# Feed-forward: the second matrix by two-by-two blocks, seven block products for eight, for four of its eleven pairs of row tiles

## The chip, the cores and the metric

The kernel runs on one NeuronCore of a Trainium2 chip. The metric is the device time of one execution in microseconds (us); the kernel before takes 1118.28 us (median of three runs, 1118.25 to 1118.4). The engines are called as the profile calls them: PE (TensorE), PEld (its weight loads), DVE (VectorE), ACT (ScalarE), POOL (GpSimd), SP (SyncE, which issues the DMAs).

## What is computed

Two layers on a sequence of 256 tokens, 1024 wide. Each layer is feed-forward, mixer, feed-forward, each followed by a layer norm; the mixer of the first layer is a hybrid of two recurrent branches, that of the second a sparse attention. So there are six stages: feed-forward, hybrid mixer, feed-forward, feed-forward, sparse attention, feed-forward. The change is in the feed-forward, which the reference writes as

```python
def swiglu(x, w_in, w_out):
    gate, up = jnp.split(x @ w_in, 2, axis=-1)
    return (jax.nn.silu(gate) * up) @ w_out

h = layer_norm(DEEPNORM_ALPHA * h + 0.5 * swiglu(h, ffn_w_in[layer, 0], ffn_w_out[layer, 0]), ...)
```

`w_in` is 1024 x 5632 (gate and up, 2816 columns each), `w_out` is 2816 x 1024. All is fp32.

## The kernel before

**Precision.** A matrix product of fp32 values is made of three products of a rounded type (fp32r): each operand is split into `hi` (rounded) and `lo` (the rest), and `mm3` issues hi·hi, hi·lo and lo·hi into one PSUM bank. `split` makes the two halves: `hi` is a copy that the planner may give to ACT or to DVE (an `alts` entry), `lo` is a subtraction on DVE. Weights come by DMA into a tile `raw` (4 buffers of 1 MB, each 128 x 2048) and are split into `whi` and `wlo`, tiles of 128 x 1024 out of a pool `m4` of 36 buffers, which nearly all other large tiles share.

**The feed-forward (`ffn`).** The 2816 inner columns are 22 row tiles `f` of 128 (NF = 22), taken in pairs `s` = 0 to 10. For each `f`, `proj_two` makes the gate and the up projection, one after the other, each into one of two PSUM banks `ps`: 8 matmuls of 512 columns and 8 of 256. `add_two` reads a bank (an ACT copy of one half, a DVE addition of the other), ACT applies silu, DVE multiplies, and the result is split into a pair tile `g` (hi and lo, 256 tokens each). Then `out_mm` multiplies `g` with two row tiles of `w_out`: for each token half b (128 tokens) and each output half c (512 columns) one `mm3` into one of the four banks `acc[b][c]`, 3 matmuls of 128 x 128 by 512 columns; 12 matmuls for a row tile, 24 for a pair. The products of a pair are issued in turn with the projections of the next. For the last `LAG` = 5 row tiles (8 in the last stage) the products of b = 1 are kept back to the end of the stage, so that the layer norm of b = 0 (`then(0, acc)`) can run beneath them.

**The layer norm** of a half reads `acc` into a tile `h` with `scalar_tensor_tensor` (0.5 · acc + `ah`, the scaled input), takes statistics, scales, and `transpose_half` transposes `h` through a bank `mp` (two of these) and splits it into the next stage's `x`. PSUM is full: 2 `ps`, 2 `mp`, 4 `acc`.

**The order.** Nothing is issued as it is written. `Plan` records each operation, and `order` sorts them by a list schedule: for each engine the operation that can start first, and among those the one recorded earliest. It has its own prices, knows the dependencies and the buffers, and gives `m4` buffers by stream under `QUOTAS`: stream W (weights) may hold 12 buffers while an earlier tile of another stream still waits for one, else 24; stream G (the tiles `g`) 4. `emit` then issues the sorted operations from one line, so that in the profile of before every operation stands at L538 (L540 in the changed file) and tiles, not lines, tell them apart. Tile names: `raw`, `whi`, `wlo` weights; `x` stage input; `ps`, `mp`, `acc` PSUM banks; `sg`, `g` feed-forward products; `h`, `lnst`, `lnmv`, `lnve`, `lng`, `lnb` layer norm.

Of the kernel before, what the change touches and what calls it, by code (L numbers as in the profile page):

```python
# [18 lines left out]
P = 128  # L19
T = 256  # L20
D = 1024
# [10 lines left out]
    "ps": (2, "PSUM"), "mp": (2, "PSUM"), "acc": (4, "PSUM"),  # L32
}

QUOTAS = {"M": None, "D": None, "S": (8, 8), "Z": (4, 4), "L": (4, 4), "G": (4, 4), "P": (5, 5), "Q": (5, 5), "W": (12, 24)}

KEPT = ("L", "G")

SHARE = {"tensor": 1.0}

# [6 lines left out]
}  # L47

ENDS = 3

STRANDS = ("mp",)
W_HYB, W_NSA = (60.0, 140.0, 25.0, 40.0, 15.0), (70.0, 60.0, 40.0, 20.0)
# [509 lines left out]
class K:  # L562
# [3 lines left out]
    def __init__(self, plan, ins, caps):  # L566
        self.nc = self.plan = plan
        self.i = ins
        self.caps = caps
        self.strand = ""  # L570
        self.consts()


# [20 lines left out]
        return v  # L594

    def m4(self, n, name, stream="M", dtype=F32):
        quota = QUOTAS[stream]
# [47 lines left out]
    def unit(self, srcs, parts):  # L645

        raw = self.plan.tile("raw", [P, 2048], F32, "raw", stream="W")
        for dst, src in srcs:
            self.nc.sync.dma_start(dst(raw), src)
        out = []  # L650
        for f in parts:
            v = f(raw)
            n = int(v.ids.size)
            shape = v.shape
            hi = self.m4(n, "whi", "W", F32R)
            lo = self.m4(n, "wlo", "W", F32R)
            if len(shape) == 3:
                hi, lo = (t.rearrange("p (a b) -> p a b", a=shape[1]) for t in (hi, lo))
            self.split(hi, lo, v)
            out.append((hi, lo))  # L660
        return out

# [38 lines left out]
    def first_weights(self, w, c0, arrivals):  # L701

        out = []
        for k0 in range(0, KD, 2):
            if k0 % 4 == 0:
                raw = self.plan.tile("raw", [P, 2048], F32, "raw", stream="W")
            v = H3(raw[:, k0 % 4 * 512:(k0 % 4 + 2) * 512], 2)
            hi, lo = (H3(self.m4(1024, n, "W", F32R), 2) for n in ("whi", "wlo"))
            step = 1 if arrivals and k0 < 4 else 2
            for e in range(0, 2, step):  # L710
                self.nc.sync.dma_start(v[:, e:e + step], w[:, k0 + e:k0 + e + step, c0:c0 + 512])
                self.split(hi[:, e:e + step], lo[:, e:e + step], v[:, e:e + step])
# [219 lines left out]
    def ffn(self, l, j, x, then, last=False):  # L932
# [8 lines left out]
        def gtiles(f):  # L941
            if f // 2 not in pairs:
                pairs[f // 2] = self.m4(1024, "g", "G", F32R).rearrange("p (a t) -> p a t", a=4)
            v = pairs[f // 2]
            return v[:, f % 2 * 2, :], v[:, f % 2 * 2 + 1, :]

        def out_mm(b, f, g, wo, cols=range(2)):
            for c in cols:
# [2 lines left out]
                self.mm3(acc[b][c], (g[0][:, bs], g[1][:, bs]), (wo[0][:, cs], wo[1][:, cs]), f == 0,  # L951
                         f == NF - 1 - (ENDS if last and b == 1 and c == 1 else 0))
        gts = {}
        if self.first:
            self.first_steps(x, w_in, gtiles, gts)
        else:
# [30 lines left out]
        for s in range(NT, DFF // 256):  # L987
            wg = self.unit_cols(w_in, s * 256, 256)
            wu = self.unit_cols(w_in, DFF + s * 256, 256)
            if s == NT:  # L990
                for n in range(NT):
                    wo = self.unit_rows(w_out, 2 * n, 2, 0, D)
                    todo += [(2 * n + e, gts[2 * n + e], wo[e]) for e in range(2)]
            if s == NT + 4:
                self.mark = len(self.plan.ops) - 1
            for e in range(2):
                if e == 1:
                    wo = self.unit_rows(w_out, 2 * s, 2, 0, D)
                f = 2 * s + e
                sg, up = self.pair("sg")  # L1000
                self.add_two(sg, self.proj_two(x, wg[e]))
                nc.scalar.activation(sg, sg, AF.Silu)
                self.add_two(up, self.proj_two(x, wu[e]))
                nc.vector.tensor_tensor(sg, sg, up, OP.mult)
                g = gtiles(f)
                self.split(g[0], g[1], sg)
                if e == 0:
                    hold = (f, g)
                    flush(1)
                else:  # L1010
                    todo.append((*hold, wo[0]))
                    flush(1)
                    todo.append((f, g, wo[1]))
        flush(0)
        then(0, acc)

        ends = late[-ENDS:] if last else []
        for c in range(2):
# [1065 lines left out]
```

## Time and profile before

| | |
|---|---|
| device time, median of 3 runs | 1118.28 us (1118.25 to 1118.4) |
| span of the profiled execution, first to last instruction | 1116.8 us, 1.5 us below the median; the page gives no other time for it |
| PE busy | 1103.7 us (99%), 6545 matmuls |
| DVE busy | 886.6 us (79%) |
| ACT busy | 516.6 us (46%) |
| DMA | 196.80 MB by the SP queue, 53.4% of 16 engines |
| the four feed-forward stages in the trace | 0 to 193 us, 430 to 615, 615 to 800, 925 to the end |

The profile page is read from its first two parts (busy shares) to the chain that ended last: followed back from the last instruction, it tells which engine's work, and of which tiles, the time goes through. Matmuls are pipelined, so that the duration of one (about 0.39 us) is longer than the distance from one to the next; for sums the distance counts, and it is read from stretches of the chain with a count. The same holds, less strongly, on DVE and ACT.

### The profile page before, as it was taken

To read this page: it belongs to the slowest core of one execution; us is meant where nothing else is said; L and a number is where in the kernel's file an instruction comes from. 1 tells how busy PE (TensorE), PEld (TensorE's weight loads), DVE (VectorE), ACT (ScalarE), POOL (GpSimd) and SP (SyncE) were. 2 spreads that over 40 slices of the span, in tenths; PEclk is the share of its full clock that TensorE was granted. 3 is DMA by queue.
4 is the path that set the end of the run, shared out by engine and by line. 5 is a ranking of instruction groups with operands and counts; after the bars stand their busy time and mean duration, and the time that the engine had idled before them with its cause. 6 is when DMAs were issued, how large, how long until landed. Compare 5 with 4: busy or idle time off the path is not lost.

```text
span 1116.8 us, 16492 instructions
## 1 busy us (share of the span) xinstructions
PE 1103.7 (99%) x6545; PEld 944.8 (85%) x6545; DVE 886.6 (79%) x1494; ACT 516.6 (46%) x932; POOL 56.2 (5%) x103
## 2 busy tenths in 40 slices
PE   9999999999999999999999999999999999999997
PEld 7888888899999788888888888888887778888886
DVE  7977768799979999777767977876879979677765
ACT  5635332278736545533433643332456776433320
POOL 1000000012001410000000000000000100000000
PEclk9999999999999999999999999999999999999999
DMA  9876562642923276755664665655426237656511
GB/s 341 302 253 197 184 216 80 188 133 55 271 96 103 88 237 215 264 188 185 193 185 155 230 210 184 211 181 163 141 91 224 76 114 266 224 188 201 176 39 38
DMA packets 147846, 197.84 MB, mean 177 GB/s; under 512 B 9373, under 2 KB 122682, under 8 KB 147770
## 3 DMA queue, kind: packets, MB, share of 16 engines
q1 hardware_dynamic: 147770, 196.80, 53.4%
q8 instruction: 51, 0.84, 0.3%
q14 instruction: 25, 0.20, 0.1%
HBM read 194.04 MB, written 1.05 MB: 175 GB/s over the span
## 4 chain that ended last, share of the span: by engine, by line
PE 87%; DVE 8%; ACT 2%; issue 2%; DMA 1%; POOL 1%; DVEq 0%; ACTq 0%; POOLq 0%
PE ps L538 52%; PE acc L538 31%; PE mp L538 4%; DVE wlo L538 2%; DVE arena L538 1%; DVE cv L538 1%; DMA raw<-in_nsa_w_in_dram 1%; ACT whi L538 1%; DVE o L538 0%; POOL arena L538 0%; DVE whi L538 0%; DVE AT L538 0%; DVE y L538 0%; DVE x L538 0%; DVE h L538 0%
## 5 line engine op out<-in xcount | busy, mean ns | idle before, releaser
L538 DVE TENSOR_TENSOR wlo<-raw,whi 128x1024 fp32r<-128x1024 f32 (+2 forms) x351 | 416.1, 1207 | 11.6 <-ACT whi L538 8.5
L538 PE MATMUL ps<-x,whi 128*128 128x512 f32 (+2 forms) x1584 | 368.8, 363 | 1.4 <-ACT cv L538 1.0
L538 PEld LDWEIGHTS ps<-x,whi 128*128 128x128 f32 (+1 forms) x1584 | 278.8, 188 | 46.1 <-ACT cv L538 3.0
L538 ACT ACTIVATE whi<-raw 128x1024 fp32r<-128x1024 f32 (+2 forms) x258 | 258.6, 1045 | 25.8 <-DMA raw<-in_ffn_w_in_dram 15.6
L538 PE MATMUL acc<-whi,g 128*128 128x512 f32 x698 | 228.5, 391 | 0.0
L538 PE MATMUL ps<-x,wlo 128*128 128x256 f32 x1368 | 222.6, 283 | 0.0
L538 ACT ACTIVATE sg<-ps 128x256 f32<-128x256 f32 x156 | 60.0, 385 | 343.9 <-PE ps L538 343.9
L538 PEld LDWEIGHTS ps<-x,wlo 128*128 128x128 f32 x1368 | 197.7, 190 | 11.3
L538 DVE TENSOR_TENSOR sg<-ps,sg 128x256 f32<-128x256 f32 (+1 forms) x158 | 67.4, 427 | 155.5 <-ACT sg L538 155.1
L538 PEld LDWEIGHTS acc<-whi,g 128*128 128x128 f32 x698 | 131.4, 188 | 25.7
L538 PE MATMUL acc<-wlo,g 128*128 128x512 f32 x349 | 136.9, 392 | 0.0
L538 PE MATMUL ps<-whi,x 128*128 128x512 f32 (+1 forms) x480 | 129.1, 385 | 0.0
L538 PEld LDWEIGHTS ps<-whi,x 128*128 128x128 f32 x480 | 85.9, 188 | 15.3 <-issue 0.8
L538 PEld LDWEIGHTS acc<-wlo,g 128*128 128x128 f32 x349 | 65.8, 189 | 10.8
L538 PE MATMUL acc<-whi,x 128*128 128x512 f32 x224 | 73.5, 404 | 0.4 <-ACT x L538 0.3
L538 PE MATMUL ps<-wlo,x 128*128 128x512 f32 (+1 forms) x240 | 67.4, 381 | 0.0
L538 DVE CAST whi<-raw 128x1024 fp32r<-128x1024 f32 (+2 forms) x93 | 63.4, 681 | 3.7 <-DMA raw<-in_nsa_w_in_dram 3.7
L538 PEld LDWEIGHTS ps<-wlo,x 128*128 128x128 f32 x240 | 43.5, 188 | 7.1
L538 PEld LDWEIGHTS acc<-whi,x 128*128 128x128 f32 x224 | 41.3, 188 | 9.5 <-DVE x L538 1.1
L538 POOL TENSOR_TENSOR lnve<-lnve,mhalf 128x1 f32<-128x1 f32 x12 | 11.5, 956 | 734.5 <-DVE lnve L538 734.5
L538 ACT ACTIVATE sg<-sg 128x256 f32<-128x256 f32 x72 | 30.2, 419 | 33.0 <-DVE sg L538 32.8
L538 PE MATMUL acc<-wlo,x 128*128 128x512 f32 x112 | 43.0, 398 | 0.0
(252 smaller groups left out, 1013.5 us busy)
## 6 DMA issues: line engine op xcount, KB each, us to landing
raw<-in_ffn_w_in_dram SPq DMA_DIRECT2D x72, 1024.0 KB, 5.2
raw<-in_ffn_w_out_dram SPq DMA_DIRECT2D x44, 1024.0 KB, 5.0
raw<-in_hyb_w_in_dram SPq DMA_DIRECT2D x20, 1024.0 KB, 5.3
raw<-in_ffn_w_in_dram SPq DMA_DIRECT2D x30, 512.0 KB, 5.0
raw<-in_hyb_w_out_dram SPq DMA_DIRECT2D x8, 1024.0 KB, 5.0
raw<-in_nsa_w_in_dram SPq DMA_DIRECT2D x5, 1024.0 KB, 5.5
raw<-in_nsa_cmp_w_dram SPq DMA_DIRECT2D x4, 1024.0 KB, 5.2
raw<-in_nsa_w_out_dram SPq DMA_DIRECT2D x4, 1024.0 KB, 6.0
```

The costliest lines, as they stand in the source:

```text
L538: r = getattr(getattr(nc, eng), fn)(*[res(a) for a in args], **{k: res(a) for k, a in kw.items()})
```

## The change

For the pairs s = 4 to 7 (`SEVEN = (4, 8)`) of every feed-forward the two row tiles and the two token halves are treated as a two-by-two block matrix, the two row tiles of `w_out` and the two output halves as another, and their product is made by the Winograd form of Strassen's method: seven block products in place of eight, of sums and differences of blocks.

- `token_forms` makes the sums of token blocks on DVE: four operations on 128 x 128 blocks of a tile `F`, then one hi copy (ACT) and one lo subtraction (DVE) of 7 blocks, 896 columns, into `fhi` and `flo`.
- `weight_forms` makes the sums of weight blocks from one `raw`: `t13` (1024 columns), two additions of 512 into `t24`, and hi and lo halves of 1024, 512, 1024 and 1024 columns. Before, a pair had hi and lo halves of 1024 and 1024.
- The products of these pairs leave the place among the projections and stand at the end of the stage in one run of 84 matmuls, in seven banks: `acc[0][0]`, `acc[0][1]`, `acc[1][0]` and the two `mp` and two `ps`. Pairs 0 to 3 stay where they were; pairs 8 to 10 (`tail`, six row tiles) follow the run, first b = 0 then b = 1, so `LAG` falls away.
- Four products were collected in banks of their own. ACT copies one, and DVE adds them up (`u`: two operations for b = 0, two for b = 1) and adds the four results to `ah` (`put`), before the layer norm reads it.
- In the feed-forward all hi halves of weights and of `g` go to ACT (`hard_split`), while before the planner chose between ACT and DVE.
- Quotas: stream W gets a limit that is written per pair (`most`), G goes from 4 to 20 buffers, and a stream F comes in.

```diff
-QUOTAS = {"M": None, "D": None, "S": (8, 8), ..., "G": (4, 4), ..., "W": (12, 24)}
-KEPT = ("L", "G")
+QUOTAS = {"M": None, "D": None, "F": None, "S": (8, 8), ..., "G": (20, 20), ..., "W": (12, 24)}
+KEPT = ("L", "G", "F")
+SEVEN = (4, 8)
...
+    def hard_split(self, hi, lo, src):
+        self.nc.scalar.activation(hi, src, AF.Copy)
+        self.nc.vector.tensor_tensor(lo, src, hi.bitcast(F32), OP.subtract)
+
+    def weight_forms(self, w, k0):
+        nc, V = self.nc, self.nc.vector
+        raw = self.plan.tile("raw", [P, 2048], F32, "raw", stream="W")
+        nc.sync.dma_start(H3(raw, 2), w[:, k0:k0 + 2, 0:D])
+        q = raw.rearrange("p (k c n) -> p k c n", k=2, c=2)
+        new = lambda name, dt=F32R: H3(self.m4(1024, name, "W", dt), 2)
+        h1, l1 = new("whi"), new("wlo")
+        self.hard_split(h1, l1, q[:, :, 0])
+        t13, t24 = new("t13", F32), new("t24", F32)
+        V.tensor_tensor(t13, q[:, 0], q[:, :, 1], OP.add)
+        b22 = new("whi")
+        self.hard_split(b22[:, 0], b22[:, 1], q[:, 1, 1])
+        h2, l2 = new("whi"), new("wlo")
+        self.hard_split(h2, l2, t13)
+        V.tensor_tensor(t24[:, 0], t13[:, 0], q[:, 1, 1], OP.add)
+        V.tensor_tensor(t24[:, 1], t24[:, 0], q[:, 1, 0], OP.add)
+        h3, l3 = new("whi"), new("wlo")
+        self.hard_split(h3, l3, t24)
...
+    def token_forms(self, F):
+        V = self.nc.vector
+        n = lambda j: F[:, j]
+        V.tensor_tensor(n(4), n(1), n(3), OP.subtract)
+        V.tensor_tensor(n(1), n(0), n(1), OP.subtract)
+        V.tensor_tensor(n(5), n(4), n(0), OP.subtract)
+        V.tensor_tensor(n(6), n(2), n(5), OP.add)
+        hi, lo = (self.m4(1024, name, "G", F32R).rearrange("p (j t) -> p j t", j=8)[:, :7] for name in ("fhi", "flo"))
+        self.hard_split(hi, lo, F[:, :7])
...
         def flush(keep):
             while len(todo) > keep:
                 f, g, wo = todo.pop(0)
                 out_mm(0, f, g, wo)
-                if f >= NF - self.LAG - (3 if last else 0):
-                    late.append((f, g, wo))
-                else:
-                    out_mm(1, f, g, wo)
+                out_mm(1, f, g, wo)
...
-                nc.vector.tensor_tensor(sg, sg, up, OP.mult)
-                g = gtiles(f)
-                self.split(g[0], g[1], sg)
-                if e == 0:
+                if seven:
+                    nc.vector.tensor_tensor(F[:, 2 * e:2 * e + 2].rearrange("p a t -> p (a t)"), sg, up, OP.mult)
+                else:
+                    nc.vector.tensor_tensor(sg, sg, up, OP.mult)
+                    g = gts[f] = gtiles(f)
+                    self.hard_split(g[0], g[1], sg)
...
+            if seven:
+                forms[s] = self.token_forms(F)
         flush(0)
+        banks = {n: self.bank(tag) for n, tag in (("b11", "mp"), ("t1", "mp"), ("t3", "ps"), ("t2", "ps"))}
+        banks.update(b21=acc[0][0], b22=acc[0][1], t4=acc[1][0])
+        for s in range(*SEVEN):
+            self.most = min(24, 20 + max(0, s - SEVEN[0] - 1) * 2)
+            w = self.weight_forms(w_out, 2 * s)
+            for n in ("b21", "b11", "b22", "t1", "t3", "t2", "t4"):
+                own = n in ("b11", "t1", "t3", "t2")
+                self.mm3(banks[n], forms[s][n], w[n], own and s == SEVEN[0], own and s == SEVEN[1] - 1)
+        tail = []
...
+        p1, us, vs, xs = u[0][:, 0], u[0][:, 1], u[1][:, 0], u[1][:, 1]
+        nc.scalar.activation(p1, banks["b11"], AF.Copy)
+        V.tensor_tensor(us, banks["t2"], p1, OP.add)
+        V.tensor_tensor(vs, banks["t1"], us, OP.subtract)
+        put(0, 0, 0.5, p1)
+        put(0, 1, 0.5, vs)
+        for f, g, wo in tail:
+            out_mm(0, f, g, wo)
+            late.append((f, g, wo))
+        self.hard = False
         then(0, acc)
+        V.tensor_tensor(us, banks["t3"], us, OP.add)
+        V.tensor_tensor(xs, banks["t1"], us, OP.subtract)
+        put(1, 0, 0.5, us)
+        put(1, 1, 0.5, xs)
```

What this does to the order is shown at three places of the second feed-forward of the first layer (the third stage, which in the trace of before ends at about 615 us).

**PE, where the last projections end.** Before, a pair's projections and products alternate, three matmuls to a bank:

```order
L538 MATMUL ps_5770<-x_4422,whi_5493 128x512 x8
L538 MATMUL ps_5770<-x_4422,wlo_5503 128x256 x8
L538 MATMUL ps_5791<-x_4422,whi_5548 128x512 x8
L538 MATMUL ps_5791<-x_4422,wlo_5551 128x256 x8
L538 MATMUL acc_4717<-whi_5448,g_5614 128x512
L538 MATMUL acc_4717<-wlo_5458,g_5614 128x512
L538 MATMUL acc_4717<-whi_5448,g_5614 128x512
L538 MATMUL acc_4725<-whi_5448,g_5614 128x512
L538 MATMUL acc_4725<-wlo_5458,g_5614 128x512
L538 MATMUL acc_4725<-whi_5448,g_5614 128x512
L538 MATMUL ps_5827<-x_4422,whi_5621 128x512 x8
```

Now all projections of the pairs from 4 on stand without a product between them, and the block products follow in one run (the start of pair 4's 21):

```order
L540 MATMUL ps_5817<-x_4489,whi_5568 128x512 x8
L540 MATMUL ps_5817<-x_4489,wlo_5584 128x256 x8
L540 MATMUL acc_4784<-whi_5582,fhi_5222 128x512
L540 MATMUL acc_4784<-wlo_5604,fhi_5222 128x512
L540 MATMUL acc_4784<-whi_5582,flo_5230 128x512
L540 MATMUL mp_5852<-whi_5582,fhi_5222 128x512
L540 MATMUL mp_5852<-wlo_5604,fhi_5222 128x512
L540 MATMUL mp_5852<-whi_5582,flo_5230 128x512
L540 MATMUL acc_4792<-whi_5624,fhi_5222 128x512 x2
L540 MATMUL acc_4792<-whi_5624,flo_5230 128x512
L540 MATMUL mp_5863<-whi_5639,fhi_5222 128x512
L540 MATMUL mp_5863<-wlo_5651,fhi_5222 128x512
```

The products moved to the end; the bank still changes every three matmuls.

**DVE, at the end of the stage.** Before, the last split of `g` is followed at once by the layer norm of b = 0, with nothing between its parts:

```order
L538 TENSOR_TENSOR g_5888<-sg_5912,g_5888 128x256
L538 SCALAR_TENSOR_TENSOR h_927_5958<-acc_4717,h_662_4353 128x512
L538 SCALAR_TENSOR_TENSOR h_927_5958<-acc_4725,h_662_4353 128x512
L538 BN_STATS lnst_5967<-h_927_5958 128x6 x2
L538 BN_AGGR lnmv_5976<-lnst_5967 128x2
L538 TENSOR_SCALAR lnve_5979<-lnmv_5976 128x1
L538 SCALAR_TENSOR_TENSOR h_927_5958<-h_927_5958,lnmv_5976,lng_5765 128x512 x2
L538 SCALAR_TENSOR_TENSOR h_927_5958<-h_927_5958,lnve_5979,lnb_5768 128x512 x2
L538 SCALAR_TENSOR_TENSOR h_934_6004<-acc_4730,h_672_4415 128x512
L538 TENSOR_TENSOR wlo_6014<-raw_5746,whi_5990 128x1024
```

Now the last split of the tail is followed by the sums `u`, the four additions to the two halves of the old `h` (`put`), and three splits of the next stage's weights:

```order
L540 TENSOR_TENSOR u_5993<-ps_5874,u_5993 128x512
L540 SCALAR_TENSOR_TENSOR h_696_4420<-u_5993,h_696_4420 128x512
L540 TENSOR_TENSOR u_6029<-mp_5863,u_5993 128x512
L540 TENSOR_TENSOR wlo_6036<-raw_5930,whi_6002 128x1024
L540 SCALAR_TENSOR_TENSOR h_696_4420<-u_6029,h_696_4420 128x512
L540 TENSOR_TENSOR u_5993<-ps_5868,u_5993 128x512
L540 TENSOR_TENSOR wlo_6050<-raw_5930,whi_6010 128x1024
L540 TENSOR_TENSOR u_6029<-mp_5863,u_5993 128x512
L540 SCALAR_TENSOR_TENSOR h_706_4482<-u_5993,h_706_4482 128x512
L540 SCALAR_TENSOR_TENSOR h_706_4482<-u_6029,h_706_4482 128x512
L540 TENSOR_TENSOR wlo_6072<-raw_5972,whi_6025 128x1024
```

and then by the layer norm of b = 0 with two more such splits inside it and one behind it:

```order
L540 SCALAR_TENSOR_TENSOR h_989_6079<-acc_4784,h_696_4420 128x512
L540 SCALAR_TENSOR_TENSOR h_989_6079<-acc_4792,h_696_4420 128x512
L540 BN_STATS lnst_6087<-h_989_6079 128x6 x2
L540 TENSOR_TENSOR wlo_6096<-raw_5972,whi_6034 128x1024
L540 BN_AGGR lnmv_6103<-lnst_6087 128x2
L540 TENSOR_TENSOR wlo_6105<-raw_5999,whi_6068 128x1024
L540 TENSOR_SCALAR lnve_6118<-lnmv_6103 128x1
L540 SCALAR_TENSOR_TENSOR h_989_6079<-h_989_6079,lnmv_6103,lng_5985 128x512 x2
L540 SCALAR_TENSOR_TENSOR h_989_6079<-h_989_6079,lnve_6118,lnb_5987 128x512 x2
L540 SCALAR_TENSOR_TENSOR h_1002_6145<-acc_4797,h_706_4482 128x512
L540 TENSOR_TENSOR wlo_6155<-raw_5999,whi_6110 128x1024
L540 TENSOR_TENSOR x_6151<-mp_6141,x_6151 128x4x128
```

**PE, at the transposes of b = 0.** Before, eight products of b = 1 stand behind the second four transposes, ahead of the first matmul that reads the new `x`:

```order
L538 MATMUL mp_6000<-ident_137,h_927_5958 128x128 x4
L538 MATMUL acc_4737<-whi_5589,g_5758 128x512
L538 MATMUL mp_6008<-ident_137,h_927_5958 128x128 x4
L538 MATMUL acc_4737<-wlo_5599,g_5758 128x512
L538 MATMUL acc_4737<-whi_5589,g_5758 128x512
L538 MATMUL acc_4737<-whi_5708,g_5888 128x512
L538 MATMUL acc_4737<-wlo_5718,g_5888 128x512
L538 MATMUL acc_4737<-whi_5708,g_5888 128x512
L538 MATMUL acc_4737<-whi_5733,g_5888 128x512
L538 MATMUL acc_4737<-wlo_5743,g_5888 128x512
L538 MATMUL acc_4737<-whi_5733,g_5888 128x512
L538 MATMUL ps_6032<-whi_5779,x_6010 128x512 x4
```

Now there is one:

```order
L540 MATMUL mp_6141<-ident_137,h_989_6079 128x128 x4
L540 MATMUL acc_4804<-wlo_6008,g_5827 128x512
L540 MATMUL mp_6149<-ident_137,h_989_6079 128x128 x4
L540 MATMUL acc_4804<-whi_5983,g_5827 128x512
L540 MATMUL ps_6160<-whi_6002,x_6151 128x512
L540 MATMUL ps_6162<-whi_6068,x_6151 128x512
L540 MATMUL ps_6160<-whi_6002,x_6151 128x512 x3
L540 MATMUL ps_6160<-whi_6010,x_6151 128x512 x4
L540 MATMUL ps_6160<-whi_6025,x_6151 128x512 x4
```

The transposes moved behind 34 of the 36 products of b = 1 that are left for the end (before: 21 of 30 stood ahead of them, counting from the end of b = 0). On PE the middle of the hybrid mixer and of the sparse attention (1036 and 566 rows in a run) stands as before.

More of the change, by code (lines that the diff above doesn't have):

```diff
@@ L570, in __init__ @@
         self.strand = ""
+        self.most, self.hard = 0, False
         self.consts()
@@ L596, in m4 @@
     def m4(self, n, name, stream="M", dtype=F32):
-        quota = QUOTAS[stream]
+        quota = (12, self.most) if stream == "W" and self.most else QUOTAS[stream]
         return self.plan.tile("m4", [P, 1024], dtype, name, stream=stream, quota=quota)[:, :n]
@@ L658, in unit @@
                 hi, lo = (t.rearrange("p (a b) -> p a b", a=shape[1]) for t in (hi, lo))
-            self.split(hi, lo, v)
+            (self.hard_split if self.hard else self.split)(hi, lo, v)
             out.append((hi, lo))
@@ L953, in ffn @@
         gts = {}
+        self.hard = True
         if self.first:
@@ L977, in ffn @@
         late = []
+        forms = {}
         def flush(keep):
@@ L982, in flush @@
                 out_mm(0, f, g, wo)
-                if f >= NF - self.LAG - (3 if last else 0):
-                    late.append((f, g, wo))
-                else:
-                    out_mm(1, f, g, wo)
+                out_mm(1, f, g, wo)
         for s in range(NT, DFF // 256):
+            self.most = min(24, 31 - 2 * (s - SEVEN[0]) if s < SEVEN[1] else 21 + SEVEN[1] - s)
             wg = self.unit_cols(w_in, s * 256, 256)
@@ L995, in ffn @@
                 self.mark = len(self.plan.ops) - 1
+            seven = SEVEN[0] <= s < SEVEN[1]
+            if seven:
+                F = self.m4(1024, "F", "F").rearrange("p (j t) -> p j t", j=8)
             for e in range(2):
-                if e == 1:
+                if e and s < SEVEN[0]:
                     wo = self.unit_rows(w_out, 2 * s, 2, 0, D)
@@ L1003, in ffn @@
                 self.add_two(up, self.proj_two(x, wu[e]))
[L1004 to L1007 removed]
+                if seven:
[4 more added lines that the diff above has]
+                    self.hard_split(g[0], g[1], sg)
+                if s >= SEVEN[0]:
+                    flush(0)
+                elif e == 0:
                     hold = (f, g)
@@ L1013, in ffn, with put @@
                     todo.append((f, g, wo[1]))
+            if seven:
+                forms[s] = self.token_forms(F)
         flush(0)
+        banks = {n: self.bank(tag) for n, tag in (("b11", "mp"), ("t1", "mp"), ("t3", "ps"), ("t2", "ps"))}
[7 more added lines that the diff above has]
+        tail = []
+        self.most = 0
+        for s in range(SEVEN[1], NF // 2):
+            wo = self.unit_rows(w_out, 2 * s, 2, 0, D)
+            tail += [(2 * s + e, gts[2 * s + e], wo[e]) for e in range(2)]
+        V = nc.vector
+        u = [H3(self.m4(1024, "u", "F"), 2) for n in range(2)]
+        side = lambda b, c: self.ah[b][:, c * 512:(c + 1) * 512]
+        def put(b, c, k, src):
+            V.scalar_tensor_tensor(side(b, c), src, k, side(b, c), OP.mult, OP.add)
+        p1, us, vs, xs = u[0][:, 0], u[0][:, 1], u[1][:, 0], u[1][:, 1]
[8 more added lines that the diff above has]
+        self.hard = False
         then(0, acc)
+        V.tensor_tensor(us, banks["t3"], us, OP.add)
+        V.tensor_tensor(xs, banks["t1"], us, OP.subtract)
+        put(1, 0, 0.5, us)
+        put(1, 1, 0.5, xs)
         ends = late[-ENDS:] if last else []
```

6 lines of the change are left out of this document (5 added, 1 removed).

## The prediction

> **What bounds the kernel now.** I read the page first: the busy shares, the granted clock and the chain that ended last.
>
> ```profile
> span 1116.8 us, 16492 instructions
> PE 1103.7 (99%) x6545; PEld 944.8 (85%) x6545; DVE 886.6 (79%) x1494; ACT 516.6 (46%) x932; POOL 56.2 (5%) x103
> PEclk9999999999999999999999999999999999999999
> PE 87%; DVE 8%; ACT 2%; issue 2%; DMA 1%; POOL 1%; DVEq 0%; ACTq 0%; POOLq 0%
> ```
>
> PE is busy through the whole span at the full clock, and 87% of the chain is its own work. DVE is the only other engine that comes near. An average says nothing of a stage, so next come the chain and the windows inside the third stage, which computes pairs 1 and 2 here; the first row of the windows is the whole stage (columns: length, then busy time and count of PE, PEld, DVE, ACT, POOL, granted clock, DMA share, GB/s).
>
> ```profile
> 644.62 8.19 PE acc L538 x36
> 652.81 5.56 PE ps L538 x32
> 658.37 2.75 PE acc L538 x12
> 661.12 5.56 PE ps L538 x32
> 615.19:800.39 185.20, 185.20 (x963) 158.58 (x962) 139.04 (x226) 74.55 (x120) 2.38 (x4) 1.00 0.58 190
> 661.00:680.50 19.50, 19.50 (x106) 16.91 (x105) 13.95 (x20) 6.17 (x10) 0.00 (x0) 1.00 0.52 168
> ```
>
> Each piece of the chain begins where the one before ended (644.62 + 8.19 = 652.81, + 5.56 = 658.37, + 2.75 = 661.12): products (`acc`) and projections (`ps`) in turn, PE to PE, no wait of another engine between. PE is busy 185.20 of 185.20 us. So the feed-forward is bound by the number of matmuls, and the distance between two products of 512 columns is 2.75/12 = .2292 us or 8.19/36 = .2275 us.
>
> **The change: what is removed.** A pair has 8 block products of 3 matmuls; four pairs now have 7. That is 3 x 4 pairs x 4 stages = 48 matmuls of 512 columns fewer (about 6497 in the profile), all on the path: 48 x .2275 to 48 x .2292 = **10.9 to 11.0 us**, 2.75 per stage. The remaining products only move.
>
> [...]
>
> **What is added on DVE and ACT.** The rows by kind of operation (busy, mean ns):
>
> ```profile
> L538 DVE TENSOR_TENSOR wlo<-raw,whi 128x1024 fp32r<-128x1024 f32 x340 | 407.5, 1220 | 11.5 <-ACT whi L538 8.5
> L538 DVE CAST whi<-raw 128x1024 fp32r<-128x1024 f32 x89 | 61.5, 691 | 3.7 <-DMA raw<-in_nsa_w_in_dram 3.7
> L538 DVE TENSOR_TENSOR g<-sg,g 128x256 fp32r<-128x256 f32 x72 | 30.6, 425 | 2.4
> L538 DVE CAST g<-sg 128x256 fp32r<-128x256 f32 x70 | 20.6, 294 | 2.4
> L538 DVE TENSOR_TENSOR arena<-mp,m_le 128x128 f32<-128x128 f32 x4 | 1.1, 282 | 0.5 <-PE mp L538 0.5
> L538 DVE TENSOR_TENSOR x<-mp,x 128x512 fp32r<-128x512 f32 x30 | 19.8, 684 | 0.2
> L538 DVE SCALAR_TENSOR_TENSOR h<-acc,h 128x512 f32<-128x512 f32 x24 | 16.4, 685 | 8.7 <-PE acc L538 8.7
> L538 DVE TENSOR_TENSOR sg<-ps,sg 128x256 f32<-128x256 f32 x156 | 66.1, 424 | 155.1 <-ACT sg L538 155.1
> L538 ACT ACTIVATE whi<-raw 128x1024 fp32r<-128x1024 f32 x251 | 253.7, 1054 | 21.9 <-DMA raw<-in_ffn_w_in_dram 11.7 <-DMA raw<-in_nsa_w_in_dram 7.9 <-DMA raw<-in_ffn_w_out_dram 2.3
> ```
>
> On DVE a pair of the sevens gets `t13` (1.22), one more lo half of 1024 and one of 512 (1.22 + .68), two additions of 512 into `t24` (2 x .68), four differences of 128 columns (4 x .28) and `flo`, 896 columns, between the rows of 128 and 1024 at 1.09; it loses two subtractions into `g` (2 x .425): 5.8 us, and 93 for 16 pairs. Each stage gets four `u` and four `put` (4 x .68 + 4 x .69 = 5.5): 22 in all. Off DVE go the feed-forward's hi copies: 70 of `g` (20.6) and 68 of the 89 of `whi` (47). The sum is +47, to about **935 us (84%)**. ACT takes these copies and the added hi halves, about +130 to 645 (58%). Neither engine passes PE; what is left is whether a piece comes late at one place. There are three.
>
> **Place 1, the projections.** With the products gone, PE asks for a bank every 2.78 us without a break (5.56 for two banks), where before a pair had 5.5 us of products between. These are a bank's hand-over in the trace, and the landing of `w_out`:
>
> ```profile
> 600.56 2.00 PE L538 MATMUL ps<-x,whi 128*128 128x512 f32 x8
> 600.76 0.38 ACT L538 ACTIVATE sg<-ps 128x256 f32<-128x256 f32 x1 [2.82 <-PE ps L538]
> 601.17 0.42 DVE L538 TENSOR_TENSOR sg<-ps,sg 128x256 f32<-128x256 f32 x1 [1.34 <-ACT sg L538]
> raw<-in_ffn_w_out_dram SPq DMA_DIRECT2D x44, 1024.0 KB, 5.0
> ```
>
> A full bank is free 601.17 + .42 - 600.56 = 1.03 us after its last matmul; the next use is 2.78 after it, so DVE may come 1.7 us late. Per pair PE needs 4 x 2.78 = 11.1 us. DVE has four reads of banks (1.70), two multiplications (.85), four lo halves of `w_in` (4.88) and, for pairs 4 to 7, the differences and `flo` (2.2): 9.7; for pairs 8 to 10 two subtractions into `g` in their place: 8.3. The weight forms of a pair (three lo halves and `t13` at 1.22, one of 512 and the two additions at .68: 6.9) fill what is left. In the order the operations of DVE between two bank reads come to at most 3.3 us against 2.78, 1.3 over where two such follow each other, below the 1.7. Cost: nothing; the cover gone, a late read costs what it exceeds 1.7 by.
>
> **Place 2, the run of 84.** It takes PE 84 x .229 = 19.3 us. By the order and these durations DVE stands inside the forms of pair 6 when it starts, and has those of pair 7 about 12.3 us into it. PE comes to pair 7 after 63 products, at 14.4, and to the last of its forms (`t24`'s halves) at about 18 us; the first it takes, `h1` and `l1`, are formed first. The tail's splits follow from 13.4 to 19.1 us, against a use from 19.5 on. So the cover is about 5 us, the cost nothing. The raws land 5.0 us after issue, on a queue with nothing else urgent.
>
> **Place 3, the ends of the stages.** Here is the end before, on the path of the layer norm of b = 0:
>
> ```profile
> 606.98 1.37 DVE L538 SCALAR_TENSOR_TENSOR h<-acc,h 128x512 f32<-128x512 f32 x2 [1.34 <-PE acc L538]
> 608.27 1.28 DVE L538 BATCH_NORM_STATS2 lnst<-h 128x6 f32<-128x512 f32 x2
> 609.89 1.40 DVE L538 SCALAR_TENSOR_TENSOR h<-h,lnmv,lng 128x512 f32<-128x512 f32 x2
> 611.21 1.41 DVE L538 SCALAR_TENSOR_TENSOR h<-h,lnve,lnb 128x512 f32<-128x512 f32 x2
> 612.23 0.60 PE L538 MATMUL mp<-ident,h 128*128 128x128 f32 x4
> 612.54 0.68 DVE L538 SCALAR_TENSOR_TENSOR h<-acc,h 128x512 f32<-128x512 f32 x1
> 613.14 1.21 DVE L538 TENSOR_TENSOR wlo<-raw,whi 128x1024 fp32r<-128x1024 f32 x1
> 614.27 1.28 DVE L538 TENSOR_TENSOR x<-mp,x 128x512 fp32r<-128x512 f32 x2
> 615.19 3.80 PE L538 MATMUL ps<-whi,x 128*128 128x512 f32 x16
> 615.47 0.68 DVE L538 BATCH_NORM_STATS2 lnst<-h 128x6 f32<-128x512 f32 x1
> ```
>
> Here start-to-start distances count: 1.13 for a lo half (613.14 to 614.27), .60 for a sum from PSUM (two in 614.27 to 615.47), .645 for a `h<-acc` (two in 606.98 to 608.27). Set the end of the run of 84 to zero. DVE has four `u` (2.4), four `put` (2.6) and three lo halves (3.4): 8.4 us. The 36 products of b = 0 end at 8.25, so the layer norm begins at 8.4, hardly late. It takes 5.25 us from its first operation to its first transpose (606.98 to 612.23), with the two interleaved lo halves 7.5: the first half is ready at 15.9, the second .65 later. PE arrives after 34 products of b = 1, (36 + 34) x .229 = 16.05: no wait for the first, about .1 for the second, which comes after four transposes and a product. Then the cover is short. Before, eight products stood behind the transposes; now one, and two matmuls of the next projections that read only the hi half of the first transposes. PE is through them at about 17.85 (four transposes and a product take .67, twice, and two matmuls .46). DVE must still do `h<-acc` (.645), a lo half (1.13) and the lo half of `x` (.60), from about 16.0 to 16.2: ready at 18.4 to 18.6, with .2 of signal (600.56 to 600.76). So PE waits **.45 to .75 us**, at the end of the third stage and of the first, which has the same order. Into the sparse attention the order holds seven covering products and its splits are narrower: 0 to .2. The last stage has no next: 0. Together **1.3 us**. Bounds: 0, if the lo halves run as their start-to-start distances and a little of slack appears; 3 us at each of three ends, 9, if the layer norm begins behind a late `u`.
>
> The profiled time is 1.5 us below the median (1118.28 - 1116.8), which I carry over. Sum: -11.0 + 1.3 = -9.7: span 1107.1, time **1108.6 us**.
>
> **Rivals.** *The ends cost more.* The sums stand ahead of the layer norm on DVE; two us at three ends: 1118.3 - 11.0 + 6 = 1113.3. For it: DVE has no idle time there in the order. Against: 36 products of b = 0 run beneath.
>
> *Slower: the forms aren't ready.* If DVE is more than about 5 us behind the place I give it when the run of 84 starts, PE is fed form by form: DVE needs 6.9 us for a pair, PE 21 x .229 = 4.8. Four pairs at 2.1, and 2.3 for the first: 10.7 lost a stage, 2.75 won, net +32 over four: 1150. For it: the window quoted above has DVE at 13.95 of 19.50 us already, and 35 us of weight forms and sums come to a stage that has 139 of 185. Against: the added operations net of the copies are 12 a stage, which leaves (139 + 12)/182.5 = 83%, and the order has two of four pairs formed before the run.
>
> [...]
>
> *No gain.* The products removed could have run under something that ends at the same time: 1118.3. The unbroken chain and PE's 185.20 of 185.20 us speak against it.
>
> **How the numbers follow.** My forecast .78; ends .10; forms late .06; clock .02; no gain .04. What this kernel can tell from no change is about .2%, 2.2 us. Faster: .78 + .10 = .88; same .04; slower .08. The range: below, all of 11.0 and no wait, 1107.3, less .3 for the spread; above, to the second case, 1113.5.
>
> **What would show it.** The page after: about 6497 matmuls, the clock row unchanged, DVE near 935, ACT near 645. The first transposes of b = 0 at the ends of the stages, earlier by 2.75 for each stage passed, later by .65 for each such end: 612.23 - 5.5 + .65 = 607.4 in the third. PE waiting on DVE `x` by .45 to .75 us at two ends. It is wrong if waits on `wlo`, `t13`, `t24` or `flo` stand inside the run of 84, if PE waits on `sg` between projections, or if the ends cost over 2 us.

## The result and the profile after

| | before | changed |
|---|---|---|
| device time, median | 1118.26 us (1118.18 to 1118.4, 4 runs) | **1110.42 us** (1109.98 to 1111.28, 4 runs) |
| span of the profiled execution | 1116.8 us | 1108.6 us |

The ratio is 0.9931, 95% interval 0.9917 to 0.9945: 7.8 us less. The prediction was 1108.6, 9.7 less, with a range of 1107.0 to 1113.5.

The page of the changed kernel, in the lines that answer to those shown of before:

```profile
span 1108.6 us, 16690 instructions
PE 1093.8 (99%) x6497; PEld 936.2 (84%) x6497; DVE 915.2 (83%) x1515; ACT 638.5 (58%) x1091; POOL 56.2 (5%) x103
PEclk9999999999999999999999999999999999999999
```

The 48 matmuls are gone (6545 to 6497); the clock row is unchanged, the mean of the span .998 as before. Its chain of waits can be followed back only to 790 us, so that the waits of PE tell more. From the view of all waits of PE these are the rows of the changed kernel that differ from before (engine and tile that waited, whom for: us in total, times, longest):

```profile
PE ps L540 <- DVE sg L540: 1.0, 2, 0.5
PE ps L540 <- DVE x L540: 0.9, 2, 0.4
PE mp L540 <- ACT arena L540: 0.5, 1, 0.5
PE mp L540 <- DVE h L540: 0.5, 1, 0.5
```

and of before:

```profile
PE mp L538 <- DVE arena L538: 1.0, 1, 1.0
PE ps L538 <- DVE sg L538: 0.3, 1, 0.3
```

The rest of the list is the same in both to .1 us. None of the new waits stands inside the run of 84 products, and none is longer than .55 us. The window of this run in the third stage, with its clock in the third figure from the right:

```profile
574.50:594.40 19.90, 19.90 (x93) 16.63 (x92) 18.68 (x23) 14.06 (x17) 0.00 (x0) 1.00 0.47 152
```

In the last stage the projections that the change left without products run in one piece, the longest of the chain (start, length, count):

```profile
992.67 72.60 PE ps L540 x416
```

In this trace a wait cost more than its row says. From start to start, over this distance and the next and against those of undisturbed matmuls, the .55 on `sg` at 87 us cost .82, each of the two on `x` .71, the one on `h` .63. The ledger, by where the same matmuls start in both traces:

| place | won | lost |
|---|---|---|
| 48 products | 11.0 | |
| opening of the kernel, before 11 us | | .4 |
| first stage, `sg` at 30 and 87 us | | .9 |
| ends of the first and third stage, `x` | | 1.4 |
| end of the fourth stage, `h` | | .6 |
| sparse attention, the wait on `arena` shorter | .6 | |
| after the last matmul | | .3 |
| **span** | **8.2** (rounded terms: 8.0) | |

From span to median 1.8 us are added where before added 1.5.

On DVE, the operations that the change brought and, in the last row, the hi copies of 1024 columns that it left there (89 before; groups by kind):

```profile
L540 DVE TENSOR_TENSOR wlo<-t,whi 128x1024 fp32r<-128x1024 f32 x32 | 39.1, 1221 | 13.8 <-ACT whi L540 13.8
L540 DVE TENSOR_TENSOR t<-t,raw 128x512 f32<-128x512 f32 x32 | 22.0, 687 | 0.3
L540 DVE TENSOR_TENSOR t<-raw 128x1024 f32<-128x1024 f32 x16 | 19.5, 1218 | 0.0
L540 DVE TENSOR_TENSOR flo<-F,fhi 128x896 fp32r<-128x896 f32 x16 | 17.4, 1090 | 2.6 <-ACT fhi L540 2.6
L540 DVE TENSOR_TENSOR F<-F 128x128 f32<-128x128 f32 x64 | 17.1, 287 | 1.0
L540 DVE CAST whi<-raw 128x1024 fp32r<-128x1024 f32 x21 | 15.0, 712 | 2.3 <-DMA raw<-in_nsa_w_in_dram 2.3
```

### The profile page after: what moved, and what is told of

It reads as the page before. It is cut to its first block, busy times and chain, and to the rows that moved or that the text cites. A ratio compares the mean times of both kernels' runs of the same rounds, so it can differ in the third digit from the quotient of the medians.

```text
span 1108.6 us, 16690 instructions
## 1 busy us (share of the span) xinstructions
PE 1093.8 (99%) x6497; PEld 936.2 (84%) x6497; DVE 915.2 (83%) x1515; ACT 638.5 (58%) x1091; POOL 56.2 (5%) x103
## 5 line engine op out<-in xcount | busy, mean ns | idle before, releaser
L540 DVE TENSOR_TENSOR wlo<-raw,whi 128x1024 fp32r<-128x1024 f32 (+3 forms) x335 | 396.9, 1205 | 51.3 <-ACT whi L540 50.2
L540 ACT ACTIVATE whi<-raw 128x1024 fp32r<-128x1024 f32 (+2 forms) x329 | 324.0, 1019 | 45.3 <-DMA raw<-in_ffn_w_in_dram 22.3
L540 PEld LDWEIGHTS ps<-x,whi 128*128 128x128 f32 (+1 forms) x1584 | 275.8, 188 | 44.2 <-ACT cv L540 3.0
L540 PE MATMUL acc<-whi,g 128*128 128x512 f32 x442 | 140.6, 391 | 0.0
L540 PEld LDWEIGHTS acc<-whi,g 128*128 128x128 f32 x442 | 83.0, 188 | 16.7
L540 PE MATMUL acc<-wlo,g 128*128 128x512 f32 x221 | 86.6, 392 | 0.0
L540 DVE TENSOR_TENSOR wlo<-t,whi 128x1024 fp32r<-128x1024 f32 x32 | 39.1, 1221 | 13.8 <-ACT whi L540 13.8
L540 PEld LDWEIGHTS acc<-wlo,g 128*128 128x128 f32 x221 | 41.6, 188 | 7.8
L540 ACT ACTIVATE whi<-t 128x1024 fp32r<-128x1024 f32 x32 | 33.9, 1059 | 23.7 <-DVE t L540 23.0
```

Of the source, the lines that this page charges most:

```text
L540: r = getattr(getattr(nc, eng), fn)(*[res(a) for a in args], **{k: res(a) for k, a in kw.items()})
```

## The experiments

Times are medians, each beside runs of the kernel before on the same chip (1118.0 to 1118.1). The diffs are against the changed kernel. Where a time is within about 2 us of the changed kernel's, the intervals of the two ratios overlap (e2, e5, e9), and the traces have to decide.

**The price of a product.**

```diff
             for n in ("b21", "b11", "b22", "t1", "t3", "t2", "t4"):
                 ...
+            self.mm3(acc[1][1], forms[s]["t4"], w["t4"], False, False)
```

> The eighth block product is put back as work alone: behind the seven of each pair stand three more matmuls of 512 columns (the t4 product once more, into the bank acc[1][1], which the tail starts afresh, so that its sum is dropped). No DVE, ACT or DMA operation is added. Theory A (every product removed lay on the path at .2275 to .2292 us): 48 more matmuls cost 10.9 to 11.0 us, 1110.4 to 1121.4. Rival B (the run of the sevens waits for its forms, or something else ends at the same time, so that the products were not what was saved): less than 3 us, 1110.4 to 1113.

Measured 1120.21 us, ratio to before 1.0019 (1.0009 to 1.0028): 9.8 us for the 48 matmuls. In one point the expectation has the edit wrong: `acc[1][1]` is started by the products of pair 0 and not by the tail, so that the extra product stays in the sum and the output is not the reference's. As work it is what was meant, 12 matmuls a stage and nothing on DVE, ACT or DMA. The trace says why not 11: of the changed kernel's waits on `x`, 1.4 us with their after-effect, none is left, presumably because 12 more matmuls per stage leave DVE the time. The one on `h` stayed (.6). 9.8 + 1.4 = 11.2: theory A, the products lay on the path.

**The hi copies back to the planner.**

```diff
     def hard_split(self, hi, lo, src):
-        self.nc.scalar.activation(hi, src, AF.Copy)
-        self.nc.vector.tensor_tensor(lo, src, hi.bitcast(F32), OP.subtract)
+        self.split(hi, lo, src)
```

> The hi copies of the feed-forward are again given to ACT or DVE by the planner (as before the change); the sevens stay. Theory A (the .55 us wait of PE on sg near 87 us in the first stage stands because hi copies are queued on ACT behind an operation that waits 5.1 us for a small DMA): the wait and its after-effect, .8 us together, go, 1109.6; DVE's busy time rises by some 40 to 70 us. Rival B (the wait has another cause): 1110.4. Rival C (DVE, at 83% already, comes late elsewhere when it gets the copies back): slower than 1111.5, with new waits on DVE in the feed-forward.

Measured 1108.35 us, ratio 0.9913 (0.9899 to 0.9928), 2.1 less than the changed kernel. The wait at 87 us is gone, which is theory A, and with the other order at the stage ends both waits on `x` are gone too, which neither theory had; the wait on `h` grew to .86. DVE went from 915 to 954 us and came late nowhere else. This is what the changed kernel does at 87 us (timeline; the table load on ACT is followed at 84.84 us by the exponential of the hybrid's rates):

```profile
83.54 1.28 ACT L540 ACT_TABLE_LOAD   x1 [5.14 <-DMA arena<-in_ssd_a_log_dram]
84.97 1.04 ACT L540 ACTIVATE whi<-raw 128x1024 fp32r<-128x1024 f32 x1
86.04 1.23 DVE L540 TENSOR_TENSOR wlo<-raw,whi 128x1024 fp32r<-128x1024 f32 x1 [6.09 <-ACT whi L540]
87.19 0.42 DVE L540 TENSOR_TENSOR sg<-ps,sg 128x256 f32<-128x256 f32 x1
87.66 2.11 PE L540 MATMUL ps<-x,whi 128*128 128x512 f32 x8 [0.55 <-DVE sg L540]
```

ACT sits 5.1 us for a small DMA. Behind it are hi copies; DVE, for want of them, sits 6.1 us; then a bank read comes late, and PE waits. In e2 the same table load waits 4.33 us, but DVE makes a hi copy itself meanwhile.

**That operation alone.**

```diff
+        self.done = len(self.plan.ops) - 1     # behind the last projection
...
-        nc.scalar.activation(rate, rate, AF.Exp)
+        with _Gate(self.plan, self.done):
+            nc.scalar.activation(rate, rate, AF.Exp)
```

> Against the changed kernel only one operation on ACT is moved: the exponential of the hybrid's rates, which in the first stage waits 5.1 us for a small DMA with the hi copies behind it, may not stand before the last projection of that stage. PE's order is the same. Theory A (this operation holds the hi copies and so the lo halves up, and PE waits .55 us on sg, .8 with its after-effect): the wait at 87 us goes, 1110.4 - .8 = 1109.6. Rival B (DVE is late there for its own load): the wait stays, 1110.4.

Measured 1110.39 us, ratio 0.9931 (0.9916 to 0.9946). The wait at 87 us is gone (theory A on the cause), and the marks of the hybrid and the third stage lie .8 to 1.0 us earlier than in the changed kernel. But the time did not move. PE's operations are the same in the same order, so that the two traces can be laid over each other, and in the fourth stage the saving is used up at two places. At 691 us .4 of it goes, where a bank read comes late: ahead of it DVE waits for another small DMA (`in_positions`), 4.3 us in the changed kernel, where PE came later and lost nothing, and an estimated 5.1 (4.3 + .8) in e9. The rest goes at the end of the stage; these are rows of the changed kernel,

```profile
784.40 2.26 ACT L540 ACTIVATE whi<-raw 128x840 fp32r<-128x840 f32 x3 [6.38 <-DMA raw<-in_nsa_w_in_dram]
785.34 1.03 DVE L540 TENSOR_TENSOR wlo<-raw,whi 128x840 fp32r<-128x840 f32 x1 [0.88 <-ACT whi L540]
786.29 1.28 DVE L540 SCALAR_TENSOR_TENSOR h<-acc,h 128x512 f32<-128x512 f32 x2
792.61 0.63 PE L540 MATMUL mp<-ident,h 128*128 128x128 f32 x4 [0.47 <-DVE h L540]
```

and these of e9:

```profile
784.54 2.26 ACT L540 ACTIVATE whi<-raw 128x840 fp32r<-128x840 f32 x3 [6.91 <-DMA raw<-in_nsa_w_in_dram]
785.48 1.03 DVE L540 TENSOR_TENSOR wlo<-raw,whi 128x840 fp32r<-128x840 f32 x1 [1.41 <-ACT whi L540]
786.43 1.28 DVE L540 SCALAR_TENSOR_TENSOR h<-acc,h 128x512 f32<-128x512 f32 x2
792.76 0.63 PE L540 MATMUL mp<-ident,h 128*128 128x128 f32 x4 [1.01 <-DVE h L540]
```

PE arrives .4 us earlier (the start less the wait: 791.75 and 792.14), the weights of the sparse attention land at the same time. In DVE's order a lo half of theirs stands ahead of the layer norm, so that the layer norm waits for a DMA, and PE for it: .47 became 1.01. Why neither DMA landed earlier too was not tried.

**The interleaved lo halves at the stage ends.** First attempt:

```diff
+        if self.ln_at is not None and not self.plan.gate and 4 <= self.los <= 8:
+            with _Gate(self.plan, self.ln_at):     # the layer norm of b = 0
+                self.nc.vector.tensor_tensor(lo, src, hi.bitcast(F32), OP.subtract)
```

> The order alone: the lo halves of the next stage from the fourth on may not stand before the layer norm of b = 0 has ended, so that none is interleaved with it. Theory A (the waits on x at the ends of the first and third stage, .43 us and about .28 of after-effect each, and the one on h into the sparse attention, .47 and .16, come of the interleaved lo halves): the first transposes come some 2.2 us earlier behind fewer products, more products cover them, and about 2.0 us go: 1108.4. Rival B (the lo halves are wanted soon after, so that the wait moves to them): 1110.4 or more, with PE waiting on wlo at the start of the next stage.

Measured 1118.92 us, ratio 1.0008 (0.9999 to 1.0017): all of the gain lost. The count had taken in three splits of `x`, so that the first five lo halves of the weights were held back, at the end of the hybrid too. The waits on `x` and `h` are gone; waits on `wlo` took their place (3.2 us in four, 2.2 of them in three at the start of the third stage), and the sparse attention with the last stage took 7.6 us more than in the changed kernel, of which more below. Second attempt, the fourth and fifth lo half of the weights, at the two ends with a wait on `x`:

```diff
+        if self.ln_at is not None and hi.t.name == "whi" and 4 <= self.los <= 5:
```

> As e4, but now only the fourth and fifth lo half of the next stage's weights are held back until the layer norm of b = 0 is through, and only at the ends of the first and the third stage (e4 counted three splits of x among its lo halves, and so held back all of the first five of the weights, at every end). Theory A (the .43 us waits on x at these two ends, .71 us each with their after-effect, come of the two interleaved lo halves): both go, 1110.4 - 1.4 = 1109.0, and no wait on wlo takes their place. Rival B (the lo halves are wanted at once by the next stage): a wait on wlo of .5 us or more at either end, 1110 or more.

Measured 1109.2 us, ratio 0.9919 (0.9904 to 0.9934), 1.2 less than the changed kernel: theory A's number, and the trace bears its mechanism out. The end of the third stage in the changed kernel,

```profile
602.82 1.29 DVE L540 SCALAR_TENSOR_TENSOR h<-acc,h 128x512 f32<-128x512 f32 x2
605.21 1.21 DVE L540 TENSOR_TENSOR wlo<-raw,whi 128x1024 fp32r<-128x1024 f32 x1
606.46 1.18 DVE L540 TENSOR_TENSOR wlo<-raw,whi 128x1024 fp32r<-128x1024 f32 x1
610.29 0.60 PE L540 MATMUL mp<-ident,h 128*128 128x128 f32 x4
610.86 1.22 DVE L540 TENSOR_TENSOR wlo<-raw,whi 128x1024 fp32r<-128x1024 f32 x1
611.99 1.28 DVE L540 TENSOR_TENSOR x<-mp,x 128x512 fp32r<-128x512 f32 x2
612.73 3.70 PE L540 MATMUL ps<-whi,x 128*128 128x512 f32 x15 [0.43 <-DVE x L540]
```

and in e5:

```profile
602.56 1.28 DVE L540 SCALAR_TENSOR_TENSOR h<-acc,h 128x512 f32<-128x512 f32 x2
607.98 0.60 PE L540 MATMUL mp<-ident,h 128*128 128x128 f32 x4
608.63 1.22 DVE L540 TENSOR_TENSOR wlo<-raw,whi 128x1024 fp32r<-128x1024 f32 x1
609.76 1.28 DVE L540 TENSOR_TENSOR x<-mp,x 128x512 fp32r<-128x512 f32 x2
611.38 3.79 PE L540 MATMUL ps<-whi,x 128*128 128x512 f32 x16
```

The layer norm takes 5.4 us to the transposes instead of 7.5, products cover the splits of `x`, and the next projections begin without a wait.

**How far ahead DVE is in the run of 84.**

```diff
         self.hard_split(h3, l3, t24)
+        V.tensor_tensor(l3, t24, h3.bitcast(F32), OP.subtract)     # e7: twice
```

> The last lo half of each of the sevens' weight forms (1024 columns, DVE) is computed twice, 16 operations of 1.13 to 1.22 us more, 4.5 to 4.9 us per stage; nothing else. Theory A (place 2 of the prediction: DVE is some 5 us ahead in the run of 84): hidden, 1110.4 within .7. Rival B (DVE is already the limit in the run): each counts in full, 16 x 1.13 = 18 us, 1128.

> The same lo half computed three times, 32 operations more, 9.0 to 9.8 us per stage. Theory A (some 5 us of slack): about 4 us per stage are not covered, 1110.4 + 16 = 1126, with PE waits on DVE in the run or in the tail. Rival B (DVE the limit already): 36 us, 1146. Rival C (slack of 9 us or more, because the planner moves other splits out of the way): 1110.4 to 1112.

Measured 1116.48 us for one (ratio 0.9990, 0.9981 to 1.0) and 1131.59 for two (1.0122, 1.0107 to 1.0137). Both numbers lie between the theories, and the traces have to be read by stage (that of e6 is of its fastest run, 1115.49). With one more, no wait stands in the run of 84 or in the tail of any stage, and the first three stages are together 2.1 us shorter than in the changed kernel (last transposes of the third at 619.7 instead of 621.8, with no wait on `x`). The fourth stage begins with waits on `wlo`, and the sparse attention with the last stage is 5.6 us longer, of which more below. So 4.5 us are hidden in the run. With two, each stage has waits in the tail, as here in the third,

```profile
597.38 0.50 PE L540 MATMUL acc<-wlo,g 128*128 128x512 f32 x1 [0.48 <-DVE wlo L540]
599.65 0.19 PEld L540 LDWEIGHTS acc<-wlo,g 128*128 128x128 f32 x1 [0.36 <-DVE wlo L540]
```

and the first stage (with the hybrid) and the third are 2.1 us longer each. By this the cover is 9.0 - 2.1, about 7 us; the rest of the 21 us is the fourth stage (6.9) and the sparse attention with what follows (10.8), in both of which the clock fell as well (last section).

**The order of the sparse attention.** In the traces of before, e1, e2, e3, e5, e9 and e11, 900 matmuls or more in a run, around the core of the sparse attention, come in the order of the changed kernel (tiles and shapes from 760 to 960 us, buffer numbers left out). In e4, e6, e7 and e8 no more than 140 in a run do: an edit upstream, and the list schedule went another way. In e10 the order alone is changed, by the number that scatters its priorities (174 matmuls in a run are left as they were):

```diff
 ORDER = {
-    4: [(180, 3.0, 8)],
+    4: [(4, 3.0, 8)],
 }
```

> Against the changed kernel only the number changes that scatters the priorities inside the sparse attention (180 to 4): the five other stages keep their order, the computation is the same, the sparse attention comes in another order. Theory A (in e4, e6, e7 and e8 the sparse attention was 6.6 to 8.5 us longer because the list schedule came out in another order there, not because of DVE's load in the feed-forward): the stretch from the last transposes of the third feed-forward to the first of the sparse attention's end, 108.0 us, gets longer by 3 to 9 us by the order alone, 1113 to 1119. Rival B (that stretch was longer for what the feed-forward left behind): within 1 us of 1110.4.

Measured 1115.45 us, ratio 0.9976 (0.9966 to 0.9986): 5.0 more than the changed kernel by the order alone, theory A in the time. The stretch that I had named is 11.4 us longer (803.7 to 923.1), more than the 3 to 9; there b = 0 comes late and b = 1 right behind it. A better measure is from the last transposes of the fourth stage to the end of the span:

| order of the core | from there to the end, us |
|---|---|
| as in the changed kernel | 304.4; e2 303.9, e5 304.1, e9 304.7, e11 303.7; with more matmuls in the last stage e3 306.3, e1 306.9, before 307.5 |
| another | e10 310.7; e6 310.0, e8 310.1, e4 312.0, e7 315.2 |

So every kernel with another order lost 5.6 us or more here, and e10 did so without any added work of DVE. A part of this can be PE's clock, which within this stretch was .68 from 869 to 872 us and .81 from 872 to 876 in e10, and .93 over 780 to 830 in e7 (last section): by what it lacks of 1.00, an estimated 1.7 and 3.5 us at most. In e4 the matmuls up to 830 us suggest it too, for how long is not shown. In e6 the mean of the whole execution is .998, as in the changed kernel, and in e8 .996. In e6 the longer stretch is all of the loss, in e4 most of it; whether the other order would have cost these the same without their own edits was not tried.

**Other numbers of pairs.**

```diff
-SEVEN = (4, 8)
+SEVEN = (4, 6)      # e3; with e2's hi copies (2, 8) in e8; with e2's and e9's edits (2, 7) in e11
```

> Only pairs 4 and 5 by sevens, five pairs in the tail. Theory A (gain by the number of products, the losses at the ends the same whatever the number of pairs): 24 more matmuls, 1110.4 + 5.5 = 1115.9. Rival B (what was lost, about 3 us, comes of DVE's added work, so that half of it goes with half the pairs): about 1114.4.

Measured 1114.24 us, ratio 0.9966 (0.9954 to 0.9979): 3.8 more, B's number, but not B's way: 24 matmuls are 5.5 us; the waits on `x` and `h` are gone whole and not by half (2.05), presumably since 60 products of b = 0 lie beneath the sums and not 36; a third wait on `sg` came. So half of the gain is lost and the price of the ends saved. The edit changes both DVE's load and the length of the tail, and does not tell the two apart.

> As e2 (hi copies to ACT or DVE as the planner chooses), with six pairs by sevens, 2 to 7, in place of four; the tail is the same. Theory A (gain by the number of products while DVE keeps up): 24 matmuls fewer than e2, 1108.35 - 5.5 = 1102.9. Rival B (DVE, then at some 91% of the span, comes late with forms or bank reads): more than 1105, with waits of PE on DVE in the feed-forward.

Measured 1126.73 us, ratio 1.0078 (1.0062 to 1.0095): theory B, and worse: 18.4 more than e2, 4.2 by the hybrid, 6.5 by the end of the third stage, 12.4 by that of the fourth, and 6 in the sparse attention and after it, whose order is another one. DVE is at 88%, and is late in three of the four feed-forwards: PE waits 1.65 us for a read of a bank in the first stage, behind the table load of e9, and in the first, the third and the fourth it waits in the run of products and once in the tail, as here in the third:

```profile
593.63 0.50 PE L540 MATMUL acc<-whi,fhi 128*128 128x512 f32 x1 [0.28 <-DVE whi L540]
595.97 0.50 PE L540 MATMUL mp<-wlo,fhi 128*128 128x512 f32 x1 [1.12 <-DVE wlo L540]
598.50 0.50 PE L540 MATMUL acc<-wlo,g 128*128 128x512 f32 x1 [0.20 <-DVE wlo L540]
```

> As e2 (hi copies by the planner) with e9's move, and with five pairs by sevens, 2 to 6; the tail has four pairs, so that 48 products of b = 0 run beneath the sums. Theory A (gain by the number of products, forms in time because the tail is longer): 12 matmuls fewer than e2, 1108.35 - 2.75 = 1105.6. Rival B (as with six pairs, DVE is late with forms and bank reads): 1108 or more, with waits on wlo or sg in the feed-forward.

Measured **1105.51 us**, ratio 0.9885 (0.9868 to 0.9901), 4.9 less than the changed kernel and faster than both: theory A to .1 us, but not by products alone: the .86 on `h` of e2 is gone as well, and a wait of .4 on `sg` has come at 57 us. In the waits of PE, nothing is left of `x` and `h` at the stage ends, and on `sg` there are .7 us. DVE has 973 us, the same 88% as in e8. So the share alone does not tell when DVE comes late. What differs is one pair fewer by sevens, four pairs of tail instead of three, and e9's move, which e8 lacks; which of them counts for how much was not tried.

## Why the prediction was right, and by how much not

- **What is removed: right.** 11.0 us, shown by e1 (11.2 with the waits that it covered) and not contradicted by e11 (12 fewer than e2, 2.8 us for a forecast of 2.75, other waits having changed too).
- **DVE and ACT: right.** The added groups measured what the rows of before gave: `t13` 1.218, halves 1.221, 512 columns .687, `flo` 1.090 (1.09), differences .287 (.28). The durations in the trace sum to 46 us more (957.7 to 1004.0; forecast 47); the page has only 29 more (915, not 935), because it counts overlapping time once, and what follows a lo half of 1.22 us starts 1.13 after it. ACT 638.5 against 645. Two smaller sums of the prediction are off without consequence: DVE's 9.7 us for a pair of projections is 9.6 by its terms, and the 35 us of weight forms and sums of a stage are 33 (4 x 6.9 + 5.5).
- **Place 1, "Cost: nothing": wrong by .8 us, in the first stage.** I had weighed DVE's own work between two bank reads, not what DVE waits for. With the hi copies on ACT alone, DVE stopped when ACT stopped: ACT 5.1 us for a small DMA, DVE 6.1 behind it. In the three other stages PE waits for no `sg` (the row with 72.60 us is one of them).
- **Place 2: right.** No wait in the run. The cover, put at 5 us, is above 4.5 and some 7 (e6, e7).
- **Place 3: the mechanism right, the size short.** The layer norm began 8.41 us after the end of the run (594.41 to 602.82; forecast 8.4), the first transposes came at 15.9 (15.9), and the wait on `x` was .43 at both ends (.45 to .75). Coming so near is luck in part: the working gives 18.4 - 17.85 to 18.6 - 17.85, so .55 to .75, even before its .2 of signal, while DVE began on the `h<-acc` of b = 1 at 15.85 and not at 16.0 to 16.2, and PE started .05 us after the lo half of `x` was done (612.68, 612.73). And the time lost is .71 each from start to start, .28 more than the row, which the term left out. Into the sparse attention I had 0 to .2, by narrower splits and seven covering products; it was .63, because a split there waits for a DMA, which I had not followed. 2.05 in place of 1.3.
- **The mark of the first transposes, 607.4, was wrong** (610.29). Taking 5.5 - .65 off 612.23 overlooked that of the stage's products 2 are left behind these transposes now, and before 9 were (8 of them behind the second four): PE does 250 products ahead of them where before it did 255, 5 fewer and not 12, so that they come 7 x .229 = 1.6 us later, 609.0. The other 1.3 us were lost upstream, .4 in the opening and .9 on `sg`, which the forecast had at nothing.
- **Not in the sum:** the opening (.4: its last transposes start at 11.20 instead of 10.82, and between 11.0 and 11.6 in all the experiments; a hi copy there waits longer for its DMA; why is left open), the .3 after the last matmul, and .6 won in the sparse attention. That this last one made up for a part of the losses was luck.
- **Its own signs of being wrong.** Two of them came up, in small: PE waited on `sg` between projections, and the three ends together cost 2.05 us, just over the 2 named. The third, waits inside the run of 84, did not. The sum held because the one large term was right and these are small beside it.
- **The rivals.** That the forms come late was told with the right mechanism and the wrong place: it comes true at six pairs (e8) and not at four. The clock, .02: no run shows that changes of bank lower it; the 84 matmuls in seven banks ran at 1.00 in the window shown.

## What to carry to other kernels

Count the work saved on the engine that is busy all the time at its start-to-start distance (here .229 us, where a matmul's row says .39), and then look for what each engine beside it can be held up by: with a step bound to one engine (here the hi copies to ACT) a wait of that engine can become one of those that it feeds (here 5.1 us on ACT, 6.1 on DVE, .55 on PE). A saving upstream (.8 to 1.0 us) can be gone at the next place where a DMA sets the time (e9), and another order by the list schedule can cost 5 us in a stage that nobody touched (e10), so compare stage by stage and not only the sum. Nor is one pair more always worth what the last one was: five pairs won 2.8 us over four, six lost 18, 6 of them in a stage downstream.

## What the runs showed of the hardware

In e7 and e10 a lower granted clock stands behind waits of PE. In e7 PE had work for .60 of two microseconds at 628, and four microseconds later the granted clock was .50 (windows; columns as in the prediction):

```profile
628.00:630.00 2.00, 0.60 (x2) 0.16 (x2) 2.00 (x3) 2.00 (x4) 0.00 (x0) 1.00 0.54 66
630.00:632.00 2.00, 1.40 (x4) 0.87 (x5) 2.00 (x4) 1.04 (x2) 0.00 (x0) 0.86 1.02 420
632.00:634.00 2.00, 2.00 (x6) 1.52 (x5) 1.79 (x3) 1.34 (x2) 0.00 (x0) 0.50 0.71 229
634.00:638.00 4.00, 4.00 (x19) 3.29 (x18) 3.66 (x6) 2.43 (x4) 0.00 (x0) 0.90 1.00 343
```

Over the last three windows the clock lacks .14 x 2 + .50 x 2 + .10 x 4 = 1.7 us of 1.00: an estimate of the most that was lost in matmuls behind the waits. The timeline agrees: the seven matmuls of 512 columns from 632.30 to 635.09 us, with no wait among them, start .40 us apart, 1.2 us more than at .229, and the nine from 635.45 on .239.

In e10 the clock was .68 from 869 to 872 us and .81 from 872 to 876, after PE had been busy for 3.3 of 6 us (863 to 869, one wait of 2.73): it lacks .32 x 3 + .19 x 4 = 1.7 us. In e7 it was .93 over 780 to 830, at the start of the sparse attention, with PE busy for 46.90 of the 50 us: 3.5 us. Two more runs show only the distances of the matmuls. In e8 the 15 of 512 columns from 632.92 to 637.70, behind waits of .40, 1.59 and .40 us, start .32 us apart, 1.3 us more than at .229. In e4, in the sparse attention, those of 256 columns start .20 to .21 us apart from 829.78 on, and .12 from 830.59 on. That the clock is behind these two is an estimate from the likeness to e7.

In e7 PE was busy for 2.0 of the four us ahead of 632, and its longest single wait there was 1.60 us. The length of one wait alone does not tell it here: in e6 PE waits 1.64 us at 869 and .60 at 872, and the eight matmuls of 512 columns from 873.94 on start .23 us apart, the usual distance. Nor does the work that PE lacks over a longer stretch: from 830 to 900 us of e7 it was busy for 67.41 of 70, at a clock of 1.00. So a stretch of waits can cost more than its length, and up to 1.7 us of the loss in the fourth stage of e7, and 1.3 in that of e8, may be this. The changed kernel's waits are single and at most 1.1 us long, and its clock is 1.00 in every window of 4 us from 4 to 1105 us.
